# Two stores in place of four, and the work of a tile shared differently between ScalarE and VectorE

## The chip, the core and the metric

The kernel runs on one core of a Trainium2 chip. The metric is the device time of one execution in microseconds (us); the kernel before takes 83.3 us. The "span" of a profile is about 1.8 us shorter than that time. A ratio below is of one kernel's fast runs over the other's in the same rounds, and so not quite the ratio of the medians that stand beside it.

## The reference

```python
x = np.random.randn(1024, 4096).astype(np.float32)   # 16.78 MB
mean = np.mean(x, axis=-1, keepdims=True)
return ((x - mean) ** 2).astype(np.float32)
```

16.78 MB have to come in and 16.78 MB have to go out. There is little arithmetic.

## The kernel before

A tile holds 4 rows of x on each of 128 partitions, that is 64 KiB a partition and 8 MiB in all; two tiles are the whole input. Both loads are issued at the start.

```python
for i in range(ntiles):                      # ntiles = 2, Q = 4, D = 4096
    x_tile = io.tile([P, Q * D], F32)
    nc.sync.dma_start(out=x_tile, in_=x_t[i])
...
for i in range(ntiles):
    for q in range(Q):
        row = tiles[i][:, q * D:(q + 1) * D]
        ...
        nc.vector.reduce_sum(out=neg_sum, in_=row, axis=mybir.AxisListType.X, negate=True)
        nc.vector.tensor_scalar_mul(out=neg_mean, in0=neg_sum, scalar1=inv_d)
        nc.scalar.activation(out=row, in_=row, func=Square, bias=neg_mean, scale=1.0)   # shortened
        if q % H == H - 1:                   # H = 2: a store after rows 1 and 3
            part = slice((q + 1 - H) * D, (q + 1) * D)
            nc.sync.dma_start(out=out_t[i][:, part], in_=tiles[i][:, part])
```

VectorE makes all means, ScalarE all squares, and a tile leaves in two stores of 4 MiB whose contiguous runs are 32 KiB.

## Time and profile before

| | before |
|---|---|
| time, median of the first 3 runs | 83.3 us (83.25 to 83.38) |
| VectorE busy | 35.4 us |
| ScalarE busy | 30.7 us |
| packet time of the DMA queue, share of 16 engines | 96.2% |
| first tile landed / first store issued | 22.5 / 39.46 us |
| second tile landed | 41.8 us |

Read the table from its last row upwards. Data come in until 41.8 us, and data go out as soon as a DMA engine is done with that. The two compute engines fit into the shadow of that. The lines themselves stand in the prediction, but for one window, between the first store's issue and the second landing (columns as there):

```profile
39.50:41.80 2.30, 0.71 (x3) 1.69 (x1) 0.00 (x0) 1.00 0.53 228
```

A share of 0.53 looks like idle DMA engines. It comes from the counting: the view books a packet where it starts, and by the packet records the last load packets start at 38.5 to 39.0 us and the first store packets from 40.96.

### The profile page before, as it was taken

How to read it: one execution, taken by the hardware profiler on the slowest of the kernel's cores; microseconds unless marked ns; L12 is line 12 of the kernel's file. 1: busy time of each engine (PE TensorE's matmuls, PEld its weight loads, DVE VectorE, ACT ScalarE, POOL GpSimd, SP SyncE). 2: the span in 40 equal slices, each digit the busy share in tenths (PEclk: the TensorE clock that was granted, in tenths of full speed). 3: DMA queues.
4: the chain of work that ended last, by engine and by line, in shares of the span. 5: the costliest groups of instructions: out<-in, count | busy, mean ns of one | idle time of the engine just before them, and what ended most of it. 6: DMA issues, size and time to landing. Idle time of an engine off the chain costs nothing.

```text
span 81.3 us, 79 instructions
## 1 busy us (share of the span) xinstructions
DVE 35.4 (44%) x16; ACT 30.7 (38%) x9; POOL 0.2 (0%) x4
## 2 busy tenths in 40 slices
DVE  0000000000099999999749999999920000000000
ACT  0000000000060005969699930979879980000000
POOL 0000000000000000000000000000000000000000
DMA  9399947999965999992997997997998998898990
GB/s 387 129 516 516 516 193 322 516 516 516 516 290 226 516 516 516 516 483 129 419 516 306 467 516 322 451 516 338 435 516 354 419 516 387 387 516 387 403 500 0
DMA packets 864, 33.55 MB, mean 413 GB/s; under 512 B 96, under 2 KB 96, under 8 KB 96
## 3 DMA queue, kind: packets, MB, share of 16 engines
q1 hardware_dynamic: 864, 33.55, 96.2%
HBM read 16.78 MB, written 16.78 MB: 412 GB/s over the span
## 4 chain that ended last, share of the span: by engine, by line
DMA 50%; DVE 22%; ACT 5%; ACTq 4%; SPq 0%; issue 0%
DMA x_tile<-in_x_dram 50%; DVE neg_sum L51 21%; ACT x_tile L55 5%; ACTq L95 4%; SPq L43 0%; DVE neg_mean L54 0%
## 5 line engine op out<-in xcount | busy, mean ns | idle before, releaser
L51 DVE TENSOR_REDUCE neg_sum<-x_tile 128x1 f32<-128x4096 f32 x8 | 35.0, 4413 | 24.1 <-DMA x_tile<-in_x_dram 24.1
L55 ACT ACTIVATE x_tile<-x_tile,neg_mean 128x4096 f32<-128x4096 f32 x8 | 29.4, 3704 | 13.5 <-DVE neg_mean L54 13.5
L55 ACT ACT_TABLE_LOAD x1 | 1.3, 1283 | 22.5 <-DMA x_tile<-in_x_dram 22.5
L54 DVE TENSOR_SCALAR neg_mean<-neg_sum 128x1 f32<-128x1 f32 x8 | 1.1, 148 | 0.0
L81 POOL MEMSET const-bfloat16-1.0<- 128x1 bf16 x1 | 0.1, 101 | 0.0
L81 POOL MEMSET const-uint8-127<- 128x1 uint8 x1 | 0.1, 101 | 0.0
L81 POOL MEMSET const-float32-0.0<- 128x1 f32 x1 | 0.1, 98 | 0.2 <-issue 0.2
L81 POOL MEMSET const-float32-1.0<- 128x1 f32 x1 | 0.1, 98 | 0.0
## 6 DMA issues: line engine op xcount, KB each, us to landing
out_dram<-x_tile SPq DMA_DIRECT2D x4, 4096.0 KB, 12.9
x_tile<-in_x_dram SPq DMA_DIRECT2D x2, 31.2
```

The source lines that it names most:

```text
L51: nc.vector.reduce_sum(out=neg_sum, in_=row, axis=mybir.AxisListType.X, negate=True)
L54: nc.vector.tensor_scalar_mul(out=neg_mean, in0=neg_sum, scalar1=inv_d)
L55: nc.scalar.activation(out=row, in_=row, func=mybir.ActivationFunctionType.Square, bias=neg_mean, scale=1.0,)
L81: nc = _bacc.Bacc("TRN2", target_bir_lowering=False, num_devices=1)
L95: with _tile.TileContext(nc) as tc:
```

## The change

The intent: longer store runs (64 KiB), hence half as many packets. A store then has to wait for a whole tile, so the tile must be finished sooner. For that, ScalarE makes the mean of row 3 with an accumulating activation while it would otherwise idle, and VectorE takes 7/16 of row 2's square.

```diff
-    H = 2
+    H = D * 9 // 16
...
+    def mean_on_act(row):
+        copy = scratch.tile([P, D], F32)
+        neg_mean = stats.tile([P, 1], F32)
+        nc.scalar.activation(
+            out=copy, in_=row, func=ACT.Identity, scale=-inv_d, accum_out=neg_mean
+        )
+        return neg_mean
...    (mean_on_dve and square_on_act are the old instructions, kept in program order)
     for i in range(ntiles):
-        ...
-                nc.sync.dma_start(out=out_t[i][:, part], in_=tiles[i][:, part])
+        row = [tiles[i][:, q * D:(q + 1) * D] for q in range(Q)]
+        m3 = mean_on_act(row[3])
+        m0 = mean_on_dve(row[0])
+        square_on_act(row[3], m3)
+        m1 = mean_on_dve(row[1])
+        square_on_act(row[0], m0)
+        m2 = mean_on_dve(row[2])
+        square_on_act(row[1], m1)
+        square_on_act(row[2][:, :H], m2)
+        back = row[2][:, H:]
+        nc.vector.tensor_scalar_add(out=back, in0=back, scalar1=m2)
+        nc.vector.tensor_mul(out=back, in0=back, in1=back)
+        nc.sync.dma_start(out=out_t[i], in_=tiles[i])
```

More of the change, by code (lines that the diff above doesn't have):

```diff
@@ L11 @@
 F32 = mybir.dt.float32
+ACT = mybir.ActivationFunctionType
 @with_exitstack
@@ L37 @@
     io = ctx.enter_context(tc.tile_pool(name="io", bufs=ntiles))
+    scratch = ctx.enter_context(tc.tile_pool(name="scratch", bufs=1))
     stats = ctx.enter_context(tc.tile_pool(name="stats", bufs=2 * ntiles * Q))
@@ L44, with mean_on_dve, square_on_act @@
         tiles.append(x_tile)
-    for i in range(ntiles):
-        for q in range(Q):
-            row = tiles[i][:, q * D:(q + 1) * D]
-            neg_sum = stats.tile([P, 1], F32)
-            neg_mean = stats.tile([P, 1], F32)
-            nc.vector.reduce_sum(
-                out=neg_sum, in_=row, axis=mybir.AxisListType.X, negate=True
-            )
-            nc.vector.tensor_scalar_mul(out=neg_mean, in0=neg_sum, scalar1=inv_d)
-            nc.scalar.activation(
-                out=row,
-                in_=row,
-                func=mybir.ActivationFunctionType.Square,
-                bias=neg_mean,
-                scale=1.0,
-            )
-            if q % H == H - 1:
-                part = slice((q + 1 - H) * D, (q + 1) * D)
-                nc.sync.dma_start(out=out_t[i][:, part], in_=tiles[i][:, part])
+    inorder = tc.keep_in_program_order
+    def mean_on_act(row):
[5 more added lines that the diff above has]
+        return neg_mean
+    def mean_on_dve(row):
+        neg_sum = stats.tile([P, 1], F32)
+        neg_mean = stats.tile([P, 1], F32)
+        inorder(nc.vector.reduce_sum(
+            out=neg_sum, in_=row, axis=mybir.AxisListType.X, negate=True
+        ))
+        inorder(nc.vector.tensor_scalar_mul(out=neg_mean, in0=neg_sum, scalar1=inv_d))
+        return neg_mean
+    def square_on_act(part, neg_mean):
+        inorder(nc.scalar.activation(
+            out=part, in_=part, func=ACT.Square, bias=neg_mean, scale=1.0
+        ))
+    for i in range(ntiles):
+        row = [tiles[i][:, q * D:(q + 1) * D] for q in range(Q)]
[11 more added lines that the diff above has]
+        nc.sync.dma_start(out=out_t[i], in_=tiles[i])
 _INS = ['x', 'axis']
```

## The prediction

> **What bounds the kernel now.** I read the page first: busy times, the slice rows, then the chain. VectorE and ScalarE are each busy under half of the span, while the DMA queue's packets fill 96.2% of the time of 16 engines.
>
> ```profile
> DVE 35.4 (44%) x16; ACT 30.7 (38%) x9; POOL 0.2 (0%) x4
> ...
> DMA  9399947999965999992997997997998998898990
> GB/s 387 129 516 516 516 193 322 516 516 516 516 290 226 516 516 516 516 483 129 419 516 306 467 516 322 451 516 338 435 516 354 419 516 387 387 516 387 403 500 0
> ...
> q1 hardware_dynamic: 864, 33.55, 96.2%
> ...
> DMA 50%; DVE 22%; ACT 5%; ACTq 4%; SPq 0%; issue 0%
> ```
>
> Two things mislead here. The dips in the slice rows (a 3, some 6s) look like idle DMA, but a packet is 64 or 32 KiB and takes 1.2 to 2.4 us, longer than a slice of 2.03 us or nearly so, and the view books it where it starts; the 516 GB/s beside the dips is no rate either. And the chain of work gives VectorE 22%, because it stops at the last ScalarE instruction (66.75 us) and never follows the stores to 81.3 us. So I asked for longer windows, cut at the kernel's events: first load packet, first landing, first store, second landing, last store issued (columns: window, its length, busy time of each engine, granted clock, DMA share, GB/s).
>
> ```profile
> 1.80:22.50 20.70, 0.00 (x1) 0.00 (x0) 0.00 (x0) 1.00 1.05 443
> 22.50:39.50 17.00, 17.00 (x6) 8.70 (x3) 0.00 (x0) 1.00 1.00 432
> ...
> 41.80:66.80 25.00, 17.71 (x8) 20.34 (x6) 0.00 (x0) 1.00 1.00 434
> 66.80:79.00 12.20, 0.00 (x0) 0.00 (x0) 0.00 (x0) 1.00 1.03 443
> ```
>
> Loads and stores alike run at 432 to 443 GB/s and a DMA share of 1.0. The packet records of the trace say the same without the smearing: the first load packet starts near 1.75 us, the earliest DMA engine finishes its last load packet at 40.96 us and begins its first store packet 2 ns later, the last store packet ends near 80.2 us, and its landing is seen 0.4 us after. The 16 engines never stop between. **The kernel is bound by moving 33.55 MB, end to end**; compute matters only if it delivers a store later than the DMA engines want one. How near it is to that shows in the order of time:
>
> ```profile
> 0.73 0.86 SPq L43 DMA_DIRECT2D x_tile<-in_x_dram  x2
> 22.50 8.75 DVE L51 TENSOR_REDUCE neg_sum<-x_tile 128x1 f32<-128x4096 f32 x2 [22.50 <-DMA x_tile<-in_x_dram]
> ...
> 39.46 27.65 SPq L64 DMA_DIRECT2D out_dram<-x_tile  x4
> ...
> 41.83 8.75 DVE L51 TENSOR_REDUCE neg_sum<-x_tile 128x1 f32<-128x4096 f32 x2 [1.62 <-DMA x_tile<-in_x_dram]
> ```
>
> The first load is issued at 0.73 and its first packet moves at 1.75, so issue to first packet takes 1.02 us. The first store, issued at 39.46, can therefore move from 40.48; engines come free at 40.96. **The margin is 0.48 us**, the number on which this change turns.
>
> **What the Trainium skill says.** "DMA: Bandwidth & Descriptors", section "Where 436 GB/s comes from", puts the ceiling of 16 engines at 435 GB/s. The trace agrees: a 32 KiB packet takes 1213 ns, which is 27.0 GB/s per engine and 432 for 16. The same page, "Why small descriptors are slow (HBM only)", gives each packet a fixed overhead of about 3 cycles: longer runs gain almost nothing at this size. The trace agrees: a 64 KiB packet takes 2418 ns against 2 x 1213 = 2426 for two of 32 KiB, 8 ns less. "ScalarE: Activation LUTs", section "What ACT_TABLE_LOAD costs", gives 280 ns + 0.833 ns per element for an ACTIVATE with a pointer bias, and 93 ns of overlap back to back. For 4096 elements that is 3692; the trace has 3692 to 3709, and 7.31 us for two in a row, that is 3.61 a step. "VectorE: DVE Perf Modes", section "The perf-mode tier table", has fp32 tensor_scalar at two elements a cycle (1227 ns for 2048) and fp32 tensor_tensor at one (2293 ns). The trace before has neither at size.
>
> **The change part by part.**
>
> 1. Four 4 MiB stores become two of 8 MiB. Per engine, 32 packets of 1213 ns (38.82 us) become 16 of 2418 ns (38.69 us). Gain: 0.13 us, all on the path that sets the end. Two issues of 0.34 us on the sync queue go, but they lay beside running transfers: 0.
>
> 2. Store 1 must now wait for all four rows of a tile instead of two. Under the old split four rows end at 47.4 us (40.11 + 7.31); waiting for that would leave the DMA engines idle for about 47.4 + 1.0 - 41.0 = 7.4 us. So the two compute changes exist to pay for the larger store.
>
> 3. ScalarE for tile 0, from 22.52: mean of row 3, about 3.69; 0.04 for its own semaphore (the trace has 35 ns from a reduce's end to the instruction that needs it); three full squares at 3.61 a step; the square of 2304 elements, 0.280 + 0.833 x 2.304 = 2.20. End: 22.52 + 3.73 + 10.83 + 2.20 = **39.28**. The means from VectorE (27.1, 31.6, 36.1 below) come before ScalarE asks for them. The table load that stood after the landing, at 22.55, no longer waits for it in the instruction order, so it runs while the load does. What reading out the accumulator costs I know from no row; a few tenths fit.
>
> 4. VectorE for tile 0: three times reduce then scale, now strictly one after the other, 4.41 + 0.035 and then 0.06 until the next reduce starts; the third scale ends at 22.50 + 3 x 4.45 + 2 x 0.06 + 0.15 = 36.11. Then 1792 elements: add, from the page's row (1227 - 256 x 0.52) = 1.09 us; multiply, 2293 - 256 / 0.96 = 2.03 us; two waits of 0.035. End: **39.30**. The split was plainly chosen to level the two.
>
> 5. Store 1 is issued near 39.34, or 39.6 with a dear accumulator read, against 39.46 before. With 1.02 us it can move by 40.36 to 40.6, still before 40.96. Cost: 0.
>
> 6. Tile 1 starts with its landing at 41.83 and needs the same 16.8 us: store 2 is issued near 58.7, can move from 59.7; the first engine ends store 1 at 40.96 + 8 x 2.418 = 60.30. Margin 0.6. Cost: 0.
>
> Sum: -0.13 us. Span 81.2, time 83.3 - 0.13 = **83.2 us**. VectorE busy falls a little (6 x 4.41 + 6 x 0.15 + 2 x 3.12 = 33.6) and ScalarE rises (2 x 16.7 + 1.3 = 34.7); both are hidden.
>
> **The rivals.**
>
> *The store comes late.* If an accumulating ACTIVATE costs 1 us more than a plain one, or VectorE's add runs at one element a cycle (+0.93 us), store 1 is ready near 41.3 instead of 40.96 and the DMA engines stand still for 0.3 to 0.5 us. Tile 1 would lose about as little, since its start is fixed by the load's landing and not by store 1: time 83.5 to 83.8. To lose 2% (1.7 us) the tile would have to take 2.1 us longer than I work out. Against it: five of the durations come from rows of this trace or match its rows.
>
> *Larger stores are really faster.* If the 64 KiB runs to memory beat the 32 KiB ones by several per cent, the gain could reach 1 us. Against it: 64 KiB loads and 32 KiB stores already agree within 0.4% per byte, both at the ceiling.
>
> *Freed engines count.* The printed chain blames VectorE for 22%; a reader who trusts it expects some 2 us from VectorE's two reduces fewer. Against it: no DMA gap is there to be closed.
>
> **Range and chances.** 83.2 is the packet sum. Below it only run spread (83.25 to 83.38 before) and start-up noise of the first packets remain: low end 82.8. Above it lies the late store: 83.8 covers a gap of 0.6 us. Faster by 2% would need 81.6, less than the packets alone allow: 1%. Slower by 2% needs both unknown durations badly wrong: 2%. Within: 97%.
>
> **What would show each step.** Store packets near 2418 ns, 256 of them, and the last landing about 0.1 us earlier: step 1. First store issued between 39.2 and 39.8 us and no gap between loads and stores: steps 3 to 5. The second near 58.7: step 6. Groups of about 1.09 us (add), 2.03 us (multiply) and 2.20 us (short square). The prediction is wrong if the accumulating ACTIVATE is far above 3.7 us, if the add is not in the doubled mode, or if store packets of 64 KiB cost other than twice those of 32.

## The result, and the profile after

The changed kernel took 83.24 us (median of 6 runs, 83.06 to 83.28), the kernel before 83.32 in the same rounds: ratio 0.9986, 95% interval 0.9973 to 0.9999. By the yardstick of 2% it is the same.

The page of the changed kernel, busy times, slice row of the DMA engines, queue, chain:

```profile
DVE 33.4 (41%) x16; ACT 34.7 (43%) x13; POOL 0.2 (0%) x4
...
DMA  9099956999982999992999992999997499998390
...
q1 hardware_dynamic: 576, 33.55, 96.0%
...
DMA 50%; DVE 21%; SPq 0%; issue 0%
```

VectorE and ScalarE changed by -2.0 and +4.0 us; the transfers did not: 33.55 MB in 576 packets (512 of data) instead of 864 (768 of data), at 96.0% of 16 engines instead of 96.2%. Longer windows of the same kernel, cut at its own events, show the same steady flow as before (419 against 443 at the end is again the counting at the windows' edges; by the packet records no engine pauses between 50 and 79 us):

```profile
1.80:22.50 20.70, 0.00 (x0) 0.21 (x1) 0.00 (x0) 1.00 1.03 437
22.50:39.70 17.20, 16.71 (x8) 16.72 (x6) 0.00 (x0) 1.00 0.99 427
42.00:59.00 17.00, 16.71 (x8) 16.72 (x6) 0.00 (x0) 1.00 1.00 432
59.00:79.00 20.00, 0.00 (x0) 0.00 (x0) 0.00 (x0) 1.00 0.97 419
```

The two engines are levelled to 16.71 and 16.72 us a tile, and in the last 20 us neither does anything. The groups of the new instructions (from the list of groups by shape: busy time and mean ns of one):

```profile
L54 ACT ACTIVATE copy<-x_tile 128x4096 f32<-128x4096 f32 x2 | 7.2, 3617 | 23.3 <-DMA x_tile<-in_x_dram 23.3
L69 ACT ACTIVATE x_tile<-x_tile,neg_mean 128x2304 f32<-128x2304 f32 x2 | 4.4, 2200 | 0.0
L85 DVE TENSOR_TENSOR x_tile<-x_tile 128x1792 f32<-128x1792 f32 x2 | 4.1, 2026 | 0.1
L84 DVE TENSOR_SCALAR x_tile<-x_tile,neg_mean 128x1792 f32<-128x1792 f32 x2 | 2.3, 1154 | 0.1
...
L54 ACT ACTIVATION_READ_ACCUMULATOR copy<-x_tile 128x1 f32 x2 | 0.4, 187 | 0.0
```

And the order of time around tile 0 (start, duration, then the instructions):

```profile
22.71 3.62 ACT L54 ACTIVATE copy<-x_tile 128x4096 f32<-128x4096 f32 x1 [20.70 <-DMA x_tile<-in_x_dram]
...
26.45 13.01 ACT L69 ACTIVATE x_tile<-x_tile,neg_mean 128x4096 f32<-128x4096 f32 x4
...
37.57 2.03 DVE L85 TENSOR_TENSOR x_tile<-x_tile 128x1792 f32<-128x1792 f32 x1
39.68 19.67 SPq L86 DMA_DIRECT2D out_dram<-x_tile  x2
42.05 3.62 ACT L54 ACTIVATE copy<-x_tile 128x4096 f32<-128x4096 f32 x1 [2.59 <-DMA x_tile<-in_x_dram]
```

ScalarE ends at 39.46, VectorE at 39.60, the store is issued at 39.68, before the second tile has landed at 42.05. "19.67 x2" is both store issues merged: the second is at 59.00.

### The profile page after: what moved, and what is told of

Its sections match the earlier page's. It is cut to its first block, busy times and chain, and to the rows that moved or that the text cites. A ratio compares the mean times of both kernels' runs of the same rounds, so it can differ in the third digit from the quotient of the medians.

```text
span 81.4 us, 79 instructions
## 1 busy us (share of the span) xinstructions
DVE 33.4 (41%) x16; ACT 34.7 (43%) x13; POOL 0.2 (0%) x4
## 2 busy tenths in 40 slices
DMA packets 577, 33.55 MB, mean 412 GB/s; under 512 B 65, under 2 KB 65, under 8 KB 65
## 3 DMA queue, kind: packets, MB, share of 16 engines
q1 hardware_dynamic: 576, 33.55, 96.0%
## 4 chain that ended last, share of the span: by engine, by line
DMA 50%; DVE 21%; SPq 0%; issue 0%
DMA x_tile<-in_x_dram 50%; DVE neg_sum L62 16%; DVE x_tile L85 2%; DVE x_tile L84 1%; DVE neg_mean L65 1%; SPq L46 0%
## 5 line engine op out<-in xcount | busy, mean ns | idle before, releaser
L62 DVE TENSOR_REDUCE neg_sum<-x_tile 128x1 f32<-128x4096 f32 x6 | 26.5, 4413 | 25.2 <-DMA x_tile<-in_x_dram 25.2
L69 ACT ACTIVATE x_tile<-x_tile,neg_mean 128x4096 f32<-128x4096 f32 (+1 forms) x8 | 26.0, 3323 | 0.1
L54 ACT ACTIVATE copy<-x_tile 128x4096 f32<-128x4096 f32 x2 | 7.2, 3617 | 23.3 <-DMA x_tile<-in_x_dram 23.3
L85 DVE TENSOR_TENSOR x_tile<-x_tile 128x1792 f32<-128x1792 f32 x2 | 4.1, 2026 | 0.1
L84 DVE TENSOR_SCALAR x_tile<-x_tile,neg_mean 128x1792 f32<-128x1792 f32 x2 | 2.3, 1154 | 0.1
```

What stands on the lines that cost most here:

```text
L54: nc.scalar.activation(out=copy, in_=row, func=ACT.Identity, scale=-inv_d, accum_out=neg_mean)
L62: inorder(nc.vector.reduce_sum(out=neg_sum, in_=row, axis=mybir.AxisListType.X, negate=True))
L69: inorder(nc.scalar.activation(out=part, in_=part, func=ACT.Square, bias=neg_mean, scale=1.0))
L84: nc.vector.tensor_scalar_add(out=back, in0=back, scalar1=m2)
L85: nc.vector.tensor_mul(out=back, in0=back, in1=back)
```

## The experiments

The theory ("A" in the expectations): the time is that of the packets, from the first load packet to the last store packet, and compute counts only through the moment at which a store is issued. Rival B: the small gain came from the moved compute. Rival C: the engines' work still costs time. The first four runs brought a surprise, from which theory E and three of the last four runs come.

Two numbers below are worked out from the packet records of each profile: the **idle** time per DMA engine where the loads end and the stores begin (time with fewer than 16 data packets in flight, times the number missing, over 16), and the **stretch**, by which the packets started between 38 and 44 us took longer than 2418 ns (64 KiB), 1213 ns (32 KiB) or 309 ns (8 KiB), summed and divided by 16. In the kernel before idle is 0.01 and stretch 0.02 us.

### The changed kernel again

> The changed kernel again, as the base for the runs beside it. Both theories: 83.2 us, 0.1 us under the kernel before; first store issued near 39.7 us, no idle DMA engine between the loads and the stores.

83.21 us (83.09 to 83.34), the kernel before 83.22 in the same rounds, ratio 0.9997 (0.9983 to 1.0012). First store issued at 39.53, idle 0.01. The gain of 0.1 us is not seen in these times; the two intervals overlap, and a gain of 0.13 us (0.16%) is about as large as their half-width.

### Shorter runs: 32 KiB and 8 KiB

```diff
-        nc.sync.dma_start(out=out_t[i], in_=tiles[i])
+        for k in range(n):                     # n = 2: 32 KiB runs; n = 8: 8 KiB runs
+            w = slice(k * Q * D // n, (k + 1) * Q * D // n)
+            nc.sync.dma_start(out=out_t[i][:, w], in_=tiles[i][:, w])
```

> The changed kernel with each tile stored as two transfers with 32 KiB runs, compute untouched. Theory A (the kernel is bound by moving bytes, and the 0.1 us came from 32 fewer, longer packets per two engines, 8 ns a pair): 32 packets of 1213 ns an engine again, 0.13 us slower than the changed kernel, so level with the kernel before (ratio to it 1.000). Rival B (the 0.1 us came from the compute that was moved between the engines): stays with the changed kernel, ratio 0.9986 or lower.

> The changed kernel with each tile stored as eight transfers with 8 KiB runs. It enlarges the packet overhead: theory A has a packet at 2418/8 + 7 = 309 ns, so 128 store packets an engine take 39.6 us instead of 38.7, and 14 more semaphore packets of 9 ns 0.13 us: about 1.0 us slower than the changed kernel, 84.2 us. Rival B: run length is of no account, 83.2 us. A further rival: short runs are much worse, several us.

With 32 KiB runs: 84.46 us, ratio to the kernel before 1.0138 (1.0116 to 1.0160). Neither theory has it: it is 1.2 us slower than the kernel before, which has just the same store packets. With 8 KiB: 85.10 us, ratio 1.0223 (1.0203 to 1.0243). Its packets take 309 ns, as expected, 39.55 us an engine against 38.82 for 32 KiB. That difference of 0.73 us is about what lies between the two runs (0.64), so the overhead per packet is right and something else costs both of them a further microsecond.

The order of time of the 32 KiB run shows what else was moved:

```profile
36.28 1.15 DVE L84 TENSOR_SCALAR x_tile<-x_tile,neg_mean 128x1792 f32<-128x1792 f32 x1
37.28 2.63 SPq L88 DMA_DIRECT2D out_dram<-x_tile  x2
37.47 2.03 DVE L85 TENSOR_TENSOR x_tile<-x_tile 128x1792 f32<-128x1792 f32 x1
43.28 3.62 ACT L54 ACTIVATE copy<-x_tile 128x4096 f32<-128x4096 f32 x1 [3.92 <-DMA x_tile<-in_x_dram]
```

Rows 0 and 1 were ready early, so the first store went out at 37.28, and the second tile landed at 43.28 instead of 42.05. In the packet records the 16 engines' last load packet, started at 38.6 to 39.2 us, took 3218 to 3788 ns in place of 2418 (stretch 1.03 us); every store packet took 1213 as usual and no engine was idle. In the 8 KiB run the first store was issued at 33.8 and the stretch was 0.99.

### No computation at all

```diff
-        m3 = mean_on_act(row[3])
-        ... (all means and squares)
         nc.sync.dma_start(out=out_t[i], in_=tiles[i])
```

> The changed kernel with all computation taken out (its result is wrong on purpose: it copies the input): two loads, two stores with 64 KiB runs. Theory A: the same time as the changed kernel within 0.2 us, 83.1 to 83.3, since nothing but the transfers sets the end. Rival C (the engines' work still costs something, for instance by slowing the transfers or at the start of the stores): faster than the changed kernel by 0.5 us or more.

84.58 us, ratio 1.016 (1.0139 to 1.0180): a bare copy is **slower** than either kernel that computes. Its output is wrong, which doesn't matter for the time. Its first store was issued behind the second load:

```profile
22.80 0.35 SPq L74 DMA_DIRECT2D out_dram<-x_tile  x1
```

The last load packets took 3332 to 3896 ns (stretch 1.19). Rival C falls: even less that stretch, 84.58 - 1.19 = 83.39 is not faster than the kernel that computes. So does theory A's tacit assumption that an early store is free.

**Theory E**: a store that reaches the queue before the DMA engines start their last load packet stretches that packet by about 1.1 us.

### Delaying the first store: parts undone

```diff
-    H = D * 9 // 16
+    H = D * 12 // 16          # front12; front16: H = D, VectorE's two instructions removed
```

> The changed kernel with ScalarE squaring 12/16 of row 2 and VectorE 4/16. ScalarE's last square ends 3/16 x 4096 x 0.833 ns = 0.64 us later, near 40.1, the first store is issued near 40.15 and can move at 41.17, 0.2 us after the first DMA engine is free. Theory A with a margin of 0.27 us: +0.2 us on the changed kernel, 83.4. If the margin is larger than worked out (queue deeper than 1.02 us suggests): 83.2.

> The part of VectorE undone: ScalarE squares the whole of row 2. ScalarE ends 7/16 x 4096 x 0.833 ns = 1.49 us later, near 40.95, the first store can move at 42.0, 1.05 us after the DMA engines want it; tile 1 is ready at about 61.36, when store 1 ends, and adds nothing. Theory A: +1.05 us on the changed kernel, 84.3. Rival (compute hidden whatever its split): 83.2.

83.47 us (ratio 1.0035, 1.0015 to 1.0055) and 83.60 us (1.0055, 1.0036 to 1.0074), with the kernel before at 83.24. The first stores were issued at 40.01 and 40.72, idle was 0.21 and 0.39. The direction is as expected, the size for the second is a third of it: ScalarE ended a little earlier than worked out, the engines came free over 41.06 to 41.36 and not at one moment, and a store moved 0.85 us after its issue, not 1.02. So VectorE's 7/16 of a row is worth about 0.4 us (83.60 against 83.21 to 83.24; by the ratios to the kernel before, 0.5 to 0.6).

```diff
-        m3 = mean_on_act(row[3])
+        m3 = mean_on_dve(row[3])
```

> The part of ScalarE undone: VectorE reduces row 3 as well, in the same place of its order. VectorE needs 21.4 us a tile, ends tile 0 near 44.1 (first store moves at 45.2, DMA engines idle 4.2 us) and tile 1 at 65.5 (second store moves at 66.6, 2.0 us after store 1 has left): +6.2 us, 89.5. Here VectorE and not the transfers sets the end. Rival (only the first gap counts, since the stores then fill the queue): +4.2 us, 87.5.

88.80 us, ratio 1.0672. VectorE now holds up both stores. The chain points the same way, though it stops before the stores, as in the kernel before, and proves nothing alone:

```profile
by line: DVE neg_sum L62 40.0%; DMA x_tile<-in_x_dram 25.2%; DVE x_tile L85 4.7%; DVE x_tile L84 2.7%; DVE neg_mean L65 1.4%; issue 0.4%
```

The first store was issued at 44.12, the second at 65.41; idle was 3.77 at the first and 1.89 at the second. The rival that counts only the first gap (87.5) falls.

```diff
-    H = 2
+    H = 4          # the kernel before, a store only after all four rows
```

> The kernel before with nothing changed but the stores: two with 64 KiB runs, each after all four rows of its tile. Tile 0 is done at 47.42, so the first store moves at 48.45, 7.5 us after the DMA engines are free; tile 1 is done at 66.76, about when store 1 leaves. Theory A: +7.5 - 0.13, 90.7 us. Rival (a longer run makes up for some of the wait): under 89 us.

90.27 us, ratio 1.0851. The slice row of the DMA engines (2.2 us a slice) shows the hole that the packet records have between 41.5 and 48.3 us (the row has it a little earlier, as it books packets where they start):

```profile
DMA  9299999999669999990009469999999999099990
```

The larger store alone costs 7 us, as the prediction's second step had it. These four runs check theory A by its own sum: the kernel before in the same rounds (83.24), less 0.13 for the packets, plus the idle time, gives 83.32, 83.50, 88.77 and 90.29; measured were 83.47, 83.60, 88.80 and 90.27. The sum uses the idle time measured in each run, so it shows where the time went, not that the idle time could be forecast. Nor does it test the 0.13: without it the first two fit better, the last two worse.

### Run length without the early issue

```diff
-        row = [tiles[i][:, q * D:(q + 1) * D] for q in range(Q)]
+        row = [tiles[i][:, q * D:(q + 1) * D] for q in (2, 1, 0, 3)]
         ... (the two stores of run32; the half stored first now holds the row finished last)
```

> The run length alone: two transfers a tile with 32 KiB runs as in run32, but the rows' parts are swapped so that the half stored first holds the row finished last, and both halves are issued together near 39.7 us, not one at 37.3. Theory A (8 ns a pair of packets): 0.13 us slower than the changed kernel, ratio to the kernel before 1.000. Theory E (what cost run32 1.2 us is only the early issue): the last load packets are 2418 ns again. Rival (two stores a tile with this compute cost 1.2 us whenever issued): 84.4 us, ratio 1.014.

83.26 us, ratio to the kernel before 0.9997 (0.9982 to 1.0013). The order of time has the two halves issued together, from 39.59 (the second at 39.99), and the second tile landed at 41.98:

```profile
39.59 0.82 SPq L88 DMA_DIRECT2D out_dram<-x_tile  x2
41.98 3.62 ACT L54 ACTIVATE copy<-x_tile 128x4096 f32<-128x4096 f32 x1 [2.60 <-DMA x_tile<-in_x_dram]
```

No packet is stretched (0.03). With the same number of stores of the same size, the 1.2 us went with the moment of issue. The run length itself is worth nothing that these timings can resolve.

### The copy with its first store held back

```diff
+        for part in row + [row[0][:, :n]]:        # n = 3150 (copy_late), 2120 (copy_mid)
+            inorder(nc.scalar.activation(out=part, in_=part, func=ACT.Identity, scale=1.0))
         nc.sync.dma_start(out=out_t[i], in_=tiles[i])
```

> The copy without computation (result wrong on purpose), with ScalarE copying each tile onto itself for 17 us so that the first store is issued near 39.5 us instead of 22.8. Theory E (a store that is queued before the DMA engines start their last load packet, at 38.5 to 39.3 us, stretches that packet by about 1.1 us): no stretched packet, 83.1 to 83.3 us. Rival (a copy is slower for another reason): 84.5 us as before.

> The same with 15.8 to 16.2 us of ScalarE work, first store issued near 38.6 us. A store moves 0.85 us after its issue where the engines are idle, so it reaches the queue near 39.5, after the last load packets have started. Theory E as stated: no stretched packet, 83.1 to 83.3 us. Rival E2 (it is enough that the store arrives while the last load packet runs): stretched packets on some or all engines, 83.7 to 84.5 us.

Both copy the input. Their outputs are wrong, which doesn't matter for the times. Late: 83.22 us, ratio 1.0002 (0.9982 to 1.0022), stretch 0.01; waiting has made the copy 1.3 us faster. Mid: 83.74 us, ratio 1.0061 (1.0042 to 1.0079), all 16 last load packets at 2734 to 3082 ns, stretch 0.45. The landing of the second tile in the order of time, first late, then mid:

```profile
39.43 0.35 SPq L77 DMA_DIRECT2D out_dram<-x_tile  x1
41.88 3.62 ACT L76 ACTIVATE x_tile<-x_tile 128x4096 f32<-128x4096 f32 x1 [2.47 <-DMA x_tile<-in_x_dram]
```

```profile
38.55 0.35 SPq L77 DMA_DIRECT2D out_dram<-x_tile  x1
42.43 3.62 ACT L76 ACTIVATE x_tile<-x_tile 128x4096 f32<-128x4096 f32 x1 [3.91 <-DMA x_tile<-in_x_dram]
```

So E is right that the early store is the cause: in two pairs of runs (32 KiB early and late, copy without work and late) the later issue took the cost away, and the copy in between pays a part. Where the threshold lies is less sure. If a store reaches the queue 0.85 us after its issue, the mid copy's came at 39.4, when all last load packets were running, and still cost 0.45: E's threshold is too early, as rival E2 has it. But by the same reckoning the late copy's came at 40.28, before any of them had ended (41.04), and cost nothing, which E2 does not say. The traces do not show when a store reaches the queue; shown is the cost by moment of issue.

### A small first load

```diff
-        nc.sync.dma_start(out=x_tile, in_=x_t[i])
+        for w in ((0, 2048), (2048, Q * D)) if i == 0 else ((0, Q * D),):
+            nc.sync.dma_start(out=x_tile[:, w[0]:w[1]], in_=x_t[i][:, w[0]:w[1]])
```

> The changed kernel with its first load cut in two, 8 KiB runs first and 56 KiB runs behind. The first packet of each engine took about 0.65 us more than later ones. Rival F (the first packet is slow in proportion to its size): an 8 KiB one loses 0.1 us only, so 0.5 us faster, 82.7 us. Theory A with a fixed start-up latency: no gain, 83.2 us.

83.19 us, ratio to the kernel before 0.9986 (0.9974 to 0.9998), that of the changed kernel. The first packets' slowness is not proportional to their size, as rival F had it: the 8 KiB packets together took 0.42 us an engine more than 309 ns each, and what was left of the gain was not seen at the end (idle before the stores was 0.12). No version beats both kernels.

### All first stores in one table

| run | first store issued, us | stretch, us | idle before the first store, us |
|---|---|---|---|
| copy without work | 22.80 | 1.19 | 0.00 |
| 8 KiB, early | 33.76 | 0.99 | 0.00 |
| 32 KiB, early | 37.28 | 1.03 | 0.00 |
| copy, mid | 38.55 | 0.45 | 0.00 |
| copy, late | 39.43 | 0.01 | 0.00 |
| before | 39.46 | 0.02 | 0.01 |
| small first load | 39.49 | 0.04 | 0.12 |
| changed, again | 39.53 | 0.01 | 0.01 |
| 32 KiB, late | 39.59 | 0.03 | 0.07 |
| changed | 39.68 | 0.03 | 0.08 |
| H = 12/16 | 40.01 | 0.05 | 0.21 |
| H = 16/16 | 40.72 | 0.04 | 0.39 |
| mean of row 3 on VectorE | 44.12 | 0.00 | 3.77 |
| larger stores only | 47.50 | 0.00 | 7.18 |

The last load packets start at 38.5 to 39.3 us and end, unstretched, at 40.9 to 41.7 (earliest with the small first load, whose idle time is therefore more than its issue suggests). Both kernels issue their first store in the narrow interval in which neither cost arises, or hardly. Why a waiting store stretches the load packet no run here tells; it stays open. It is not every transfer that waits in the queue: the second load is queued 20 us before the first ends, and the packets at that boundary take 2418 to 2420 ns in both kernels; nor does a later boundary between two stores show it.

## Why the prediction was right

It forecast 83.2 us and "within 2%"; 83.24 came. "The same" is a wide target, 81.7 to 85.0 us, which the early 32 KiB stores (84.46) would have met too, so the steps count for more than the number. Point by point:

- **Bound by the transfers.** Shown. The copy whose store comes at the same moment as the kernel's takes the same time (83.22), and compute that holds the store up adds just its idle time (the four sums above).
- **Step 1, 0.13 us from fewer packets.** The packets measured 2418 ns, 256 of them for the stores, as forecast. In the time the gain is at the edge of what can be seen: 0.9986 in one set of rounds, 0.9997 in the other. The sign that the prediction named, a last landing 0.1 us earlier, failed in the profiled run: it came at 80.65 us against 80.55. The last landing is that of one DMA engine. By the packet records, averaged over the 16, the loads ended at 41.25 us (41.26 before) and the stores at 80.02 (80.01): the store packets took 0.09 us less, and 0.07 us more idle time ate most of that. In the repeated run, with an idle time of 0.01, the stores ended at 79.91 on average, the 0.1 us earlier, and the last landing was at 80.52. So in these packet records the packets save about what was forecast, and which engine ends last hides it.
- **Step 2, the large store would cost some 7.4 us by itself.** Measured: 7.2 us of idle time, 90.27 us.
- **Step 3, ScalarE.** 16.76 us a tile forecast, 16.75 measured (22.71 to 39.46). The accumulator's read is an instruction of its own, 187 ns; the ACTIVATE that makes the mean (another function, no pointer bias) takes 3617 instead of 3692 ns and overlaps it, which almost cancels it.
- **Step 4, VectorE.** 16.80 us forecast, 16.89 measured (22.71 to 39.60). The add took 1154 ns and not 1090.
- **Step 5, store 1 issued at 39.34 to 39.6 at no cost.** 39.68, at 0.08 us. The work was sized well (counted from the first landing, which came 0.2 us later, the issue is where it was forecast); the margin was not. It was reckoned as 0.48 us in the kernel before, with one issue-to-packet time of 1.02 us, that of the first load. Measured, this time is no constant: 0.84 to 0.85 us on idle engines, but 1.46 us in the changed kernel, where loads were still running. Small gaps show already at an issue of 39.59, about 1.4 us before the first engine ends its loads. So in the kernel before little more than 0.1 us was left. It did not matter because the first microsecond past the margin costs little: 1.3 us later costs 0.39. At 44.12 it costs 3.77.
- **Step 6, store 2.** 59.00 against 58.7, no idle time there (0.00).
- **The rivals.** "The store comes late" was the only one that was seen, at 0.08 us. What the prediction did not consider at all was a store that comes too early: its step 5 has any issue before the margin at no cost, while one at 38.55 cost 0.45 us of stretch and one at 37.28 cost 1.03. In this change it does not happen, since both kernels issue at 39.5 to 39.7. For the prediction that was luck.

## What to carry to other kernels

Where the DMA engines never stop, as here, moving work between compute engines buys only the right to issue a store in time; read the moment of issue against the end of the loads, not the busy shares. Test such a bound with a copy, but hold its store to the kernel's moment: the copy that queued its store early was 1.3 us slower than the kernel it was to be the floor of. Where loads are followed by stores on one queue, it is worth trying a later first store and not only an earlier one.

## What the Trainium skill lacked or had wrong

- "DMA: Bandwidth & Descriptors", section "Rules for kernel authors", advises to issue a DMA early when overlapping it with compute. It lacks the case seen here: stores issued at 22.8 to 37.3 us stretched the last load packets from 2418 ns to 3100 to 3900, and cost 1.2 us (32 KiB runs) to 1.3 us (copy) of 83.
- "ScalarE: Activation LUTs", section "What ACT_TABLE_LOAD costs", gives the duration of an ACTIVATE, which the runs confirm (2200 ns for 2304 elements with a pointer bias), but no cost for its accumulator output: here a separate instruction of 187 ns.
- "VectorE: DVE Perf Modes", section "The perf-mode tier table", has 1227 ns for an fp32 tensor_scalar of 2048 elements. With a per-partition scalar the runs had 1154 ns for 1792 elements, above the 1090 estimated from this row; whether the per-partition scalar is the reason no run tells. Its fp32 tensor_tensor agrees (2026 ns for 1792 elements; estimated from its row of 2293 ns: 2026).
